# Splitting the operands of the block products on VectorE alone, the weights in whole raw tiles of 1024 columns

## The chip, the cores and the metric

The kernel runs on one core of a Trainium2 chip. Its engines work side by side, each on its own list of instructions in order: TensorE (PE in the profile, its weight loads PEld), VectorE (DVE), ScalarE (ACT), GpSimd (POOL) and SyncE (SP), whose queue here issues nearly all DMA transfers. The metric is the device time of one execution in microseconds (us); the time of a kernel is the median of its runs.

## The reference

Two layers over 1024 latent tokens of width 1024, with 256 context tokens that only the first layer needs. All is float32.

```python
# layer 0: z = h @ w_in, five parts of 1024 columns
y_a = conformer_conv(va, vg, p) * silu(ga)        # depthwise conv of 31 taps, LayerNorm, SiLU
y_b = rglru(xb, h_ctx) * silu(gb)                 # two recurrences, gates from 128x128 heads
x = x + gate * (concat([y_a, y_b]) @ w_out)
# layer 1: u, g = split(h @ w_in), 2048 columns each
d = multiscale_pool(u)                            # windows 2, 4, 8, 16 in rows of 64 tokens, minus u
y = einsum(d, w_grp) * scale                      # per group of 512 columns
x = x + gate * ((y * silu(g)) @ w_out)
return rmsnorm(x, final_g)
```

Before each layer stand an RMSNorm and a modulation by a shift and a scale. The kernel folds `w_grp` into the first half of layer 1's `w_in` (it calls the product `wfold`), and it keeps everything transposed: channels on the 128 partitions, tokens along the free axis in two halves of 512.

## The kernel before

**Three products for one.** Every float32 product is made of three TensorE products. A float32 operand is split into a high part, cast to the `float32r` type that TensorE multiplies, and a low part, the remainder. `split` (L94) does that with one ScalarE cast (L95) and one subtraction on a given engine (L96). Then hi*hi, hi*lo and lo*hi are summed in PSUM (L607, L609, L610). So each operand, weight or activation, costs one cast and one subtraction before TensorE can use it; the operands' engine is what this case is about.

**Block products.** From about the middle on the kernel multiplies by a 2x2 block scheme with seven products in place of eight. `wquad` (L569) prepares the weights of two output tiles of 128 columns at once. It loads two raw tiles of 128x1024 (tag `wr`, two buffers in all), sees them as four blocks a11, a12 and a21, a22 of 512 columns, forms sums of blocks on VectorE (L587, L588, L589, L595), partly in place, and splits seven operands p1 to p7, each from 512 columns. In the order of the code p1 and p6 are split on VectorE, and p5, p2, p7, p3, p4 on GpSimd. An operand's hi and lo parts share one tile of 128x1024. `quad` (L620) runs the products in the order p1, p5, p6, p2, p7, p3, p4 into three PSUM tiles a, c and b. `prod` (L603) makes 12 matmuls of 128x512 for each, so a quad has 84. Between the products `put` evacuates a PSUM tile, or a copy of it is kept, on ScalarE or VectorE, and the next product that adds into that tile waits for it. The factors on the token side (names b11, t1, t2, b21, t3, b22, t4) are sums of blocks too, split once and kept.

**Four uses, in the order of time.**

1. `woa` (names ending in `woa`): the half of layer 0's output projection that takes y_a, 4 quads. Its token operands are `ya_...`, split by `split_op` (L553), which takes VectorE for even i and GpSimd for odd i.
2. `v` and `g`, layer 1's input projection, for m = 0, 2, ..., 14: a quad of `wfold` weights (tiles `wq_v`) and one of `wg` weights (`wq_g`), 16 quads. Token operands `x_...` by `split_x` (L871); t1 and t4 on GpSimd, the others in a VectorE form of their own. Between them VectorE makes the pooling (`pool`, L928 to L946) of four half tiles, with 2, 4, 3 and 1 doubling steps for m = 0 and 2, 4 and 6, 8 and 10, 12 and 14. Then come the gating (L1062) and sums for the next operand (`block_sums`, L559 to L562), which are stored to memory.
3. `wo0`: the first part of layer 1's output projection, 4 quads (`wq_wo`). Its token operands `y_...` are read back from memory and split by `y_operand` (L971), each from 128x1024 columns: of a name's two tiles the first on GpSimd and the second on VectorE, except b22, both on VectorE.
4. `wo1`: the second part, 4 quads, the last two (names ending in `_l`, `late=True` in `wquad`) with the final RMSNorm worked in between.

**Buffers.** The weight operands of `v` and `g` live in the pool `xpool` (8 tiles of 128x1024), those of the other uses in a ring over the tags `wh`, `wl` (2 buffers each) and `d`. A tile is given out again when every reader of its last content is done. PSUM has 4 tiles for a, c and b.

**What sets the order.** The program is written as dataflow. A scheduler gives each engine's list its order by priorities and its own estimate of times, hands out the buffers as they come free and adds the waits. `tc.high_priority` moves evacuations ahead, and `tc.issue_after` holds some work back. A change of an operand's engine or size thus changes the order around it too.

Of the kernel before, what the change touches and what calls it, by code (L numbers as in the profile page):

```python
# [10 lines left out]
F32R = mybir.dt.float32r  # L11
# [4 lines left out]
P = 128  # L16
# [3 lines left out]
D = 1024  # L20
KT = D // P
H = 512
HALF = (slice(0, H), slice(H, S))
# [32 lines left out]
def body(ctx, tc, xT, ctxT, cc, ccol, modT, modW, win, gw, wout, wu, grp, wg, wo1, small, edge, ident, outT):  # L56
    nc = tc.nc
    mult, add, sub = ALU.mult, ALU.add, ALU.subtract
# [4 lines left out]
    wpool = ctx.enter_context(tc.tile_pool(name="wpool", bufs=2))  # L63
# [11 lines left out]
    def dtile(name, dt=F32):  # L75
        return dpool.tile([P, S], dt, tag="d", name=name)
# [4 lines left out]
    def ttile(name):  # L81
        return tpool.tile([P, H], F32, tag="t", name=name)
# [11 lines left out]
    def split(src, hi, lo, eng):  # L94
        return (nc.scalar.copy(hi, src),  # L95
                eng.tensor_tensor(out=lo, in0=src, in1=hi.bitcast(F32), op=sub))  # L96
# [161 lines left out]
    hh, hl, ch, cl = [], [], [], []  # L258
# [162 lines left out]
    with ExitStack() as actx:  # L421
# [6 lines left out]
        def ltile(name, dt=F32):  # L428
            return lpool.tile([P, E], dt, tag="l", name=name)
# [49 lines left out]
        for j in range(KT):  # L479
# [13 lines left out]
            w = wload(win[KT + j], f"vg{j}", nc.gpsimd)  # L493
            sg = []
            for h in range(2):
                ps = psum(f"vg{j}_{h}")
                mm3(ps, w, (hh, hl), HALF[h])
                t = ttile(f"sg{j}_{h}")
                nc.scalar.activation(t, ps, AF.Sigmoid)
                sg.append(t)  # L500
            w = wload(win[j], f"va{j}", nc.gpsimd)
# [13 lines left out]
            for d in range(2):  # L515
                for gi, ob in ((0, O_BR), (1, O_BI)):
                    kc = slice((2 * gi + d) * P, (2 * gi + d + 1) * P)
                    t = ltile(f"g{j}_{d}_{gi}")
# [21 lines left out]
    def vtile(name):  # L540
        return vpool.tile([P, H], F32, tag="v", name=name)
# [10 lines left out]

    def split_op(ops, name, i, src):  # L553
        hi, lo = ops[name]
        return split(src, hi[i], lo[i], nc.gpsimd if i % 2 else nc.vector)


    def block_sums(b11, b12, b21, b22, t3, eng):
# [10 lines left out]
    def wquad(src, name, ring, late=False):  # L569
        raw = []  # L570
        for i in range(2):
            r = wpool.tile([P, D], F32, tag="wr", name=f"wr_{name}_{i}")
            loaded[0] = nc.sync.dma_start(r, src[i])
            raw.append(r)
        a11, a12 = [raw[0][:, h] for h in HALF]
        a21, a22 = [raw[1][:, h] for h in HALF]

        def op(v, i, eng):
            t = ring(f"wq_{name}_{i}")
            split(v, t[:, HALF[0]], t[:, HALF[1]], eng)  # L580
            return t

        p1 = op(a11, 1, nc.vector)
        if late:
            p4 = op(a22, 4, nc.gpsimd)
        s3 = ttile(f"ws_{name}")
        nc.vector.tensor_tensor(out=s3, in0=a11, in1=a21, op=sub)  # L587
        nc.vector.tensor_tensor(out=a21, in0=a21, in1=a22, op=add)  # L588
        nc.vector.tensor_tensor(out=a11, in0=a21, in1=a11, op=sub)  # L589
        if not late:  # L590
            p5 = op(a21, 5, nc.gpsimd)
        p6 = op(a11, 6, nc.vector)
        p2 = op(a12, 2, nc.gpsimd)
        p7 = op(s3, 7, nc.gpsimd)
        nc.vector.tensor_tensor(out=a12, in0=a12, in1=a11, op=sub)  # L595
        if late:
            p5 = op(a21, 5, nc.gpsimd)
        p3 = op(a12, 3, nc.gpsimd)
        if not late:
            p4 = op(a22, 4, nc.gpsimd)  # L600
        return p1, p2, p3, p4, p5, p6, p7

    def prod(ps, w, op, first, last):  # L603
        xh, xl = op
        for k in range(KH):
            hi, lo = w[:, k * P : (k + 1) * P], w[:, H + k * P : H + (k + 1) * P]
            nc.tensor.matmul(ps, hi, xh[k], start=(first and k == 0), stop=False,  # L607
                             skip_group_check=not first)
            nc.tensor.matmul(ps, hi, xl[k], start=False, stop=False, skip_group_check=not first)  # L609
            mm = nc.tensor.matmul(ps, lo, xh[k], start=False, stop=(k == KH - 1),  # L610
                                  skip_group_check=not first)
        return mm
# [47 lines left out]
    for j in range(KT):  # L660
        w = wload(win[4 * KT + j], f"gb{j}", nc.gpsimd)
# [51 lines left out]
    for h in range(2):  # L713
        ps = wide(f"mu{h}", h)[:, :H]
        nc.tensor.matmul(ps, ones, lnacc[h][:, :H], start=True, stop=True)
        for j in range(KT):
            v = us[j][:, HALF[h]]
# [3 lines left out]
            else:  # L721
                q = ttile(f"lsq{j}_{h}")
                nc.scalar.activation(q, v, AF.Square)
                eng = nc.gpsimd if h else nc.vector
# [5 lines left out]
    for m in range(KT):  # L730
        w = wload(wout[m, 1], f"wob{m}", nc.gpsimd)
        for h in range(2):
            ps = psum(f"wob{m}_{h}")
            mm3(ps, w, (bh, bl), HALF[h])
            t = vtile(f"xp{m}_{h}")
            nc.sync.dma_start(t, xT[m][:, HALF[h]])
            with tc.high_priority(offset=EVAC):
                nc.vector.scalar_tensor_tensor(out=t, in0=ps, scalar=m0[:, 0, 2 * KT + m : 2 * KT + m + 1],
                                               in1=t, op0=mult, op1=add)
# [32 lines left out]
    for i in range(KH):  # L772
        for j in (i, KH + i):
            w = wload(win[2 * KT + j], f"ga{j}", nc.gpsimd)
            for h in range(2):
# [3 lines left out]
                v = us[j][:, HALF[h]]  # L779
                nc.vector.tensor_tensor(out=v, in0=v, in1=ps, op=mult)  # L780
        b11, b12 = [us[i][:, h] for h in HALF]
        b21, b22 = [us[KH + i][:, h] for h in HALF]
        split_op(ya, "b11", i, b11)
        split_op(ya, "b21", i, b21)
        t1, t2, t3, t4 = b11, ttile(f"yat2_{i}"), b12, b21
# [19 lines left out]
    def wo_weights(m):  # L805
        return wquad([wout[m + i, 0] for i in range(2)], f"woa{m}", ring_w)
# [49 lines left out]
    def ring_x(name):  # L856
        return xpool.tile([P, S], F32R, tag="x", name=name)

    first_ring = iter(["wh", "wl", "wh", "wl"])

    def ring_first(name):
        tag = next(first_ring, None)
        return dtile(name, F32R) if tag is None else wpool.tile([P, D], F32R, tag=tag, name=name)

    def v_weights(m, ring):
        return wquad([wfold[(m + i) // 4][(m + i) % 4].rearrange("p k c -> p (k c)") for i in range(2)], f"v{m}", ring)
# [4 lines left out]
    def split_x(name, i, src, shift, eng):  # L871
        hi, lo = bx[name]
        if shift is None:
            split(src, hi[i], lo[i], eng)
        else:
            nc.scalar.activation(hi[i], src, AF.Identity, bias=shift)
            nc.vector.scalar_tensor_tensor(out=lo[i], in0=src, scalar=shift, in1=hi[i].bitcast(F32), op0=add, op1=sub)
# [6 lines left out]
    def shift(k):  # L884
        return m1[:, 0, k : k + 1]
# [9 lines left out]
    for i in range(KH):  # L895
        b11, b21 = x1[i][:, HALF[0]], scaled(0, KH + i)
        split_x("b21", i, b21, shift(KH + i), None)
        b12, b22 = scaled(1, i), scaled(1, KH + i)
        t = block_sums(b11, b12, b21, b22, ttile(f"xt3_{i}"), nc.vector)
        split_x("t1", i, t["t1"], None, nc.gpsimd)  # L900
        split_x("t2", i, t["t2"], shift(KH + i), None)
        split_x("t3", i, t["t3"], dsh[:, i : i + 1], None)
        split_x("b22", i, b22, shift(KH + i), None)
        split_x("t4", i, t["t4"], None, nc.gpsimd)


    fin = [None, None]
# [63 lines left out]
    def y_operand(ops, part, name, raw_tile, alloc):  # L971
        hi, lo = [], []
        for q in range(2):
            r = raw_tile(f"yr_{part}_{name}_{q}")
            nc.sync.dma_start(r, y_raw[part][name][:, q * S : (q + 1) * S])
            hi.append(alloc(f"y{part}_{name}h{q}", F32R))
            lo.append(alloc(f"y{part}_{name}l{q}", F32R))
            split(r, hi[q], lo[q], nc.vector if q or name == "b22" else nc.gpsimd)
        halves = lambda ts: [t[:, h] for t in ts for h in HALF]
        ops[name] = halves(hi), halves(lo)  # L980

# [23 lines left out]
    for m in range(0, NK, 2):  # L1005
# [38 lines left out]
        elif m <= KT:  # L1044
            n = 2 * KT + m - 2
            for q in range(2):
                raw = dtile(f"mod1_{n + q}")
# [7 lines left out]
        w = quad(wq, f"g{m}", bx, to_gate, (lambda: wo1_weights(0, 0)) if m == NK - 2 else None)  # L1055
# [24 lines left out]
    for m in range(0, KT, 2):  # L1080
# [28 lines left out]
        w = quad(w, f"wo0_{m}", yops[0], put, nxt)  # L1109
# [10 lines left out]
    for m in range(0, KT - 4, 2):  # L1120
# [10 lines left out]
        w = quad(w, f"wo1_{m}", yops[1], put, ahead)  # L1131
# [99 lines left out]
    wb, _, _ = last_half0(m, wa, ahead)  # L1231
# [140 lines left out]
```

## Time and profile before

| what | value |
|---|---|
| median of 3 runs | 1459.48 us (1458.37 to 1459.95) |
| the profiled execution | 1463.59 us, its span 1461.8 us |
| busy in the span: PE, PEld | 1320.6 us (90%), 1060.1 us (73%) |
| busy in the span: DVE, ACT, POOL | 1220.5 us (83%), 653.0 us (45%), 695.8 us (48%) |
| mean granted TensorE clock | 0.959 |
| DMA | 181.79 MB, 124 GB/s over the span |

The profiled execution is one of its own: it took 4.1 us more than the median, and its span, from the first to the last instruction, is 1.8 us short of its time. Sums below are made against it. Busy time is a union, so what overlaps on one engine counts once. A group's mean mixes instructions that ran alone with those that something held up; the minimum, median and maximum of a tile's instructions tell the two apart. A wait is put down to the last semaphore that arrived.

### The profile page before, as it was taken

How to read it: one execution, taken by the hardware profiler on the slowest of the kernel's cores; microseconds unless marked ns; L12 is line 12 of the kernel's file. 1: busy time of each engine (PE TensorE's matmuls, PEld its weight loads, DVE VectorE, ACT ScalarE, POOL GpSimd, SP SyncE). 2: the span in 40 equal slices, each digit the busy share in tenths (PEclk: the TensorE clock that was granted, in tenths of full speed). 3: DMA queues.
4: the chain of work that ended last, by engine and by line, in shares of the span. 5: the costliest groups of instructions: out<-in, count | busy, mean ns of one | idle time of the engine just before them, and what ended most of it. 6: DMA issues, size and time to landing. Idle time of an engine off the chain costs nothing. (4 is left out here: it accounts for less than half of the span.)

```text
span 1461.8 us, 15776 instructions
## 1 busy us (share of the span) xinstructions
PE 1320.6 (90%) x5664; PEld 1060.1 (73%) x5664; DVE 1220.5 (83%) x1389; ACT 653.0 (45%) x928; POOL 695.8 (48%) x372
## 2 busy tenths in 40 slices
PE   7889989998899899999998998899889998889796
PEld 4478767776777677788886776677767777668585
DVE  7985889799879899997778749999999887876765
ACT  6343674475467623225424345533333334534442
POOL 5183644663666556424427435543243344654522
PEclk9899999999999999999999999999999999999998
DMA  9731112111211133443545364233323235647623
GB/s 354 253 121 37 65 37 73 51 68 40 79 51 51 64 103 106 142 141 115 168 159 174 121 194 131 86 115 131 127 75 108 101 108 137 234 162 266 237 73 115
DMA packets 82866, 181.79 MB, mean 124 GB/s; under 512 B 7778, under 2 KB 27618, under 8 KB 82788
## 3 DMA queue, kind: packets, MB, share of 16 engines
q1 hardware_dynamic: 74340, 176.60, 35.6%
q10 hardware_dynamic: 8448, 4.20, 1.0%
q8 instruction: 44, 0.72, 0.2%
q14 instruction: 34, 0.28, 0.1%
HBM read 136.72 MB, written 44.04 MB: 124 GB/s over the span
## 5 line engine op out<-in xcount | busy, mean ns | idle before, releaser
L688 DVE SCALAR_TENSOR_TENSOR conv<-u,sm,conv 128x1009 f32<-128x1009 f32 (+14 forms) x240 | 301.0, 1273 | 21.7 <-ACT conv L681 18.5
L96 POOL TENSOR_TENSOR wq_v<-wr_v,wq_v 128x512 fp32r<-128x512 f32 x32 | 54.3, 1712 | 84.6 <-ACT wq_v L95 84.4
L96 POOL TENSOR_TENSOR wq_g<-wr_g,wq_g 128x512 fp32r<-128x512 f32 x32 | 49.8, 1567 | 91.8 <-ACT wq_g L95 91.5
L96 POOL TENSOR_TENSOR wq_wo<-wr_wo,wq_wo 128x512 fp32r<-128x512 f32 x32 | 49.1, 1542 | 58.4 <-ACT wq_wo L95 48.6
L96 POOL TENSOR_TENSOR wl_wu<-wr_wu,wh_wu 128x1024 fp32r<-128x1024 f32 x16 | 39.4, 2467 | 73.6 <-ACT wh_wu L95 73.6
L95 ACT CAST wq_g<-wr_g 128x512 fp32r<-128x512 f32 x48 | 28.2, 619 | 94.7 <-DVE wr_g L588 33.9
L95 ACT CAST wq_v<-wr_v 128x512 fp32r<-128x512 f32 x48 | 28.2, 619 | 81.0 <-DVE wr_v L595 29.3
L521 PE MATMUL g<-uh,wh_gw 128*128 128x512 f32 (+1 forms) x96 | 40.7, 425 | 25.8 <-ACT g L524 16.3
L524 ACT ACTIVATE g<-g,sm 128x512 f32<-128x512 f32 (+1 forms) x96 | 53.6, 624 | 18.0 <-PE g L523 10.0
L440 POOL TENSOR_TENSOR g<-g,uc 128x1280 f32<-128x1280 f32 x16 | 47.4, 2961 | 19.6 <-ACT g L524 19.6
L243 PE MATMUL fold<-gh,wh_wu 128*128 128x512 f32 x128 | 52.7, 413 | 4.3 <-ACT wh_wu L95 4.3
L125 PE MATMUL gb<-h0h,wh_gb 128*128 128x512 f32 x128 | 51.2, 400 | 5.7 <-ACT sb L669 5.7
L244 PE MATMUL fold<-gl,wh_wu 128*128 128x512 f32 x128 | 52.5, 410 | 3.2 <-DVE gl L96 3.2
L95 ACT CAST wq_wo<-wr_wo 128x512 fp32r<-128x512 f32 x48 | 28.8, 619 | 58.9 <-DVE wr_wo L588 15.0
L445 POOL TENSOR_TENSOR g<-g,g 128x1280 f32<-128x1280 f32 x16 | 50.6, 3182 | 9.1 <-ACT g L444 9.1
L446 DVE SCALAR_TENSOR_TENSOR g<-a,g 128x1280 f32<-128x1280 f32 x16 | 37.1, 2317 | 20.4 <-POOL g L445 20.4
L245 PE MATMUL fold<-gh,wl_wu 128*128 128x512 f32 x128 | 50.9, 407 | 2.7 <-POOL wl_wu L96 2.7
L928 DVE TENSOR_TENSOR ws<-ws 128x616 f32<-128x616 f32 (+2 forms) x48 | 52.3, 1091 | 0.9
L458 POOL TENSOR_TENSOR g<-g,g 128x1024 f32<-128x1024 f32 x8 | 19.2, 2394 | 70.6 <-DVE g L455 70.6
L127 PE MATMUL va<-h0h,wl_va 128*128 128x512 f32 x128 | 49.5, 391 | 2.1 <-POOL wl_va L96 2.1
L126 PE MATMUL gb<-h0l,wh_gb 128*128 128x512 f32 x128 | 51.0, 399 | 0.0
L127 PE MATMUL gb<-h0h,wl_gb 128*128 128x512 f32 x128 | 50.8, 398 | 0.0
(566 smaller groups left out, 4744.7 us busy)
## 6 DMA issues: line engine op xcount, KB each, us to landing
mod<-modT SPq DMA_DIRECT2D x28, 512.0 KB, 5.3
wr_wu<-wu SPq DMA_DIRECT2D x16, 512.0 KB, 4.1
x_part<-xp SPq DMA_DIRECT2D x32, 256.0 KB, 2.6
mod<-modT SPq DMA_DIRECT2D x32, 256.0 KB, 3.3
wr_v<-wfold SPq DMA_DIRECT2D x16, 512.0 KB, 3.3
wr_g<-wg SPq DMA_DIRECT2D x16, 512.0 KB, 4.3
yr_t<-y_t SPq DMA_DIRECT2D x16, 512.0 KB, 6.1
wr_wo<-wo SPq DMA_DIRECT2D x16, 512.0 KB, 4.2
```

The source lines that it names most:

```text
L95: return (nc.scalar.copy(hi, src), eng.tensor_tensor(out=lo, in0=src, in1=hi.bitcast(F32), op=sub))
L96: eng.tensor_tensor(out=lo, in0=src, in1=hi.bitcast(F32), op=sub))
L125: nc.tensor.matmul(ps, hi[:, kc], xh[k][:, cols], start=(k == 0), stop=False)
L126: nc.tensor.matmul(ps, hi[:, kc], xl[k][:, cols], start=False, stop=False)
L127: nc.tensor.matmul(ps, lo[:, kc], xh[k][:, cols], start=False, stop=(k == ks - 1))
L243: nc.tensor.matmul(ps, wh[:, kc], gh[i], start=(i == 0), stop=False)
L244: nc.tensor.matmul(ps, wh[:, kc], gl[i], start=False, stop=False)
L245: nc.tensor.matmul(ps, wl[:, kc], gh[i], start=False, stop=(i == 3))
L445: nc.gpsimd.tensor_tensor(out=iu, in0=iu, in1=r, op=mult)
L524: nc.scalar.activation(t[:, a : a + n], ps[:, :n], AF.Sigmoid, bias=col(ob + d * KT + j))
L688: nc.vector.scalar_tensor_tensor(out=acp[:, a:b], in0=us[j][:, a + o : b + o], scalar=col(O_CONVW + 31 * j + k), in1=acp[:, a:b], op0=mult ...
L928: nc.vector.tensor_tensor(out=nxt[:, :, a_:b_], in0=cur[:, :, a_ + o0 : b_ + o0], in1=cur[:, :, a_ + o1 : b_ + o1], op=add)
```

## The change

All splits of the block products go to VectorE: `split_op`, the `x_t1` and `x_t4` splits, `y_operand`, and the weights in `wquad`. In `wquad` two operands are now split at once where two stand side by side in a raw tile. `both(1, raw[0])` splits the whole first raw tile into p1 and p2, `both(5, raw[1])` the second one into p5 and p4 after a21 + a22 has been formed in its first half, `both(6, raw[0])` the first tile again into p6 and p3 after both of its halves have been rewritten. Only p7 remains a split of 512 columns. The hi parts of such a pair share one tile of 128x1024 and the lo parts another, so a quad still takes seven tiles; a pair's tiles come free when both of its products are done. The two late quads keep seven splits of 512, on VectorE. The list of tags for the first quad of `v` is adapted.

```diff
     def split_op(ops, name, i, src):
         hi, lo = ops[name]
-        return split(src, hi[i], lo[i], nc.gpsimd if i % 2 else nc.vector)
+        return split(src, hi[i], lo[i], nc.vector)
 ...
-        def op(v, i, eng):
+        def op(v, i):
             t = ring(f"wq_{name}_{i}")
-            split(v, t[:, HALF[0]], t[:, HALF[1]], eng)
-            return t
-
-        p1 = op(a11, 1, nc.vector)
+            p = t[:, HALF[0]], t[:, HALF[1]]
+            split(v, *p, nc.vector)
+            return p
+
         if late:
-            p4 = op(a22, 4, nc.gpsimd)
+            p1, p4 = op(a11, 1), op(a22, 4)
+            s3 = ttile(f"ws_{name}")
+            nc.vector.tensor_tensor(out=s3, in0=a11, in1=a21, op=sub)
+            nc.vector.tensor_tensor(out=a21, in0=a21, in1=a22, op=add)
+            nc.vector.tensor_tensor(out=a11, in0=a21, in1=a11, op=sub)
+            p6, p2, p7 = op(a11, 6), op(a12, 2), op(s3, 7)
+            nc.vector.tensor_tensor(out=a12, in0=a12, in1=a11, op=sub)
+            p5, p3 = op(a21, 5), op(a12, 3)
+            return p1, p2, p3, p4, p5, p6, p7
+
+        def both(i, r):
+            hi, lo = [ring(f"wq_{name}_{i}{c}") for c in "hl"]
+            split(r, hi, lo, nc.vector)
+            return [(hi[:, h], lo[:, h]) for h in HALF]
+
+        p1, p2 = both(1, raw[0])
         s3 = ttile(f"ws_{name}")
         nc.vector.tensor_tensor(out=s3, in0=a11, in1=a21, op=sub)
         nc.vector.tensor_tensor(out=a21, in0=a21, in1=a22, op=add)
+        p5, p4 = both(5, raw[1])
         nc.vector.tensor_tensor(out=a11, in0=a21, in1=a11, op=sub)
-        if not late:
-            p5 = op(a21, 5, nc.gpsimd)
-        p6 = op(a11, 6, nc.vector)
-        p2 = op(a12, 2, nc.gpsimd)
-        p7 = op(s3, 7, nc.gpsimd)
         nc.vector.tensor_tensor(out=a12, in0=a12, in1=a11, op=sub)
-        if late:
-            p5 = op(a21, 5, nc.gpsimd)
-        p3 = op(a12, 3, nc.gpsimd)
-        if not late:
-            p4 = op(a22, 4, nc.gpsimd)
+        p6, p3 = both(6, raw[0])
+        p7 = op(s3, 7)
         return p1, p2, p3, p4, p5, p6, p7
 ...
-            hi, lo = w[:, k * P : (k + 1) * P], w[:, H + k * P : H + (k + 1) * P]
+            hi, lo = [v[:, k * P : (k + 1) * P] for v in w]
 ...
-    first_ring = iter(["wh", "wl", "wh", "wl"])
+    first_ring = iter(["wh", "wl", "d", "d", "d", "d", "wh"])
 ...
-        split_x("t1", i, t["t1"], None, nc.gpsimd)
+        split_x("t1", i, t["t1"], None, nc.vector)
 ...
-        split_x("t4", i, t["t4"], None, nc.gpsimd)
+        split_x("t4", i, t["t4"], None, nc.vector)
 ...
-            split(r, hi[q], lo[q], nc.vector if q or name == "b22" else nc.gpsimd)
+            split(r, hi[q], lo[q], nc.vector)
```

**In the order: VectorE at the weights of the g quad of m = 6.** `wr_g` are its raw tiles, `ws` and `vp` belong to the pooling, and the two rows that read `qb_v` and `qc_v` evacuate PSUM tiles of the v quad that TensorE adds into again (L1022 before, L1031 in the changed file). Before:

```order
L589 TENSOR_TENSOR wr_g_0_7583<-wr_g_1_7585,wr_g_0_7583 128x512
L928 TENSOR_TENSOR ws_0_1_7623<-vp_6540 128x8x79
L96 TENSOR_TENSOR wq_g_6_7597<-wr_g_0_7583,wq_g_6_7597 128x512
L928 TENSOR_TENSOR ws_0_2_7625<-ws_0_1_7623 128x8x77
L928 TENSOR_TENSOR ws_0_4_7627<-ws_0_2_7625 128x8x73
L595 TENSOR_TENSOR wr_g_0_7583<-wr_g_0_7583 128x512
L928 TENSOR_TENSOR ws_0_8_7629<-ws_0_4_7627 128x8x65
L937 TENSOR_TENSOR ws_0_8_7629<-ws_0_8_7629,eg 128x8x8
L941 TENSOR_TENSOR ws_0_8_7629<-ws_0_8_7629,eg 128x8x7
L946 SCALAR_TENSOR_TENSOR vp_6540<-ws_0_8_7629,vp_6540 128x8x64
L1022 TENSOR_TENSOR vp_6549<-qb_v_7480,s_v_7506 128x8x64
L1022 TENSOR_TENSOR vp_6543<-qc_v_7479,s_v_7520 128x8x64
```

And now, with the splits of whole raw tiles (`wq_g_1l`, `wq_g_5l`, `wq_g_6l`):

```order
L96 TENSOR_TENSOR wq_g_1l<-wr_g_0_7517,wq_g_1h 128x1024
L561 TENSOR_TENSOR y_7229<-y_7230,y_7229 128x512
L937 TENSOR_TENSOR ws_0_1_7551<-vp_6510 128x8x79
L606 TENSOR_TENSOR wr_g_0_7517<-wr_g_1_7519,wr_g_0_7517 128x512
L562 TENSOR_TENSOR y_7230<-y_7230,y_7229 128x512
L96 TENSOR_TENSOR wq_g_5l<-wr_g_1_7519,wq_g_5h 128x1024
L1031 TENSOR_TENSOR vp_6513<-qc_v_7413,s_v_7454 128x8x64
L937 TENSOR_TENSOR ws_0_2_7553<-ws_0_1_7551 128x8x77
L607 TENSOR_TENSOR wr_g_0_7517<-wr_g_0_7517 128x512
L1031 TENSOR_TENSOR vp_6519<-qb_v_7414,s_v_7440 128x8x64
L937 TENSOR_TENSOR ws_0_4_7555<-ws_0_2_7553 128x8x73
L96 TENSOR_TENSOR wq_g_6l<-wr_g_0_7517,wq_g_6h 128x1024
```

The two evacuations stand ahead of most of the pooling's chain now, where a whole pass of it (four sums, two edges, L946) stood ahead of them; between them stand the splits.

**GpSimd at the same place.** Before, its list held five rows for that quad:

```order
L96 TENSOR_TENSOR wq_g_5_7594<-wr_g_1_7585,wq_g_5_7594 128x512
L96 TENSOR_TENSOR wq_g_2_7600<-wr_g_0_7583,wq_g_2_7600 128x512
L96 TENSOR_TENSOR wq_g_7_7603<-ws_g_7590,wq_g_7_7603 128x512
L96 TENSOR_TENSOR wq_g_3_7607<-wr_g_0_7583,wq_g_3_7607 128x512
L96 TENSOR_TENSOR wq_g_4_7610<-wr_g_1_7585,wq_g_4_7610 128x512
```

Now it holds none from the last fold weight (`wl_wu`) and eight memsets to the last multiplications of the final norm (L1201):

```order
L96 TENSOR_TENSOR wl_wu_3_6107<-wr_wu_3_6104,wh_wu_3_6106 128x1024
L1020 MEMSET vp_6513 128x8x8
L1021 MEMSET vp_6513 128x8x8
L1020 MEMSET vp_6516 128x8x8
L1201 TENSOR_TENSOR o_0_10158<-x_1_9591,rr_10123 128x512
```

All five splits of that quad, and those of every other, have left GpSimd.

**TensorE at the start of `woa`.** Before, after the last matmuls of p1 (`wq_woa_1`) came the first two of p5, then of p6, then of p2:

```order
L610 MATMUL qa_woa_5490<-ya_b11h_4748,wq_woa_1_5423 128x512
L607 MATMUL qc_woa_5491<-ya_t1h_4751,wq_woa_5_5430 128x512
L609 MATMUL qc_woa_5491<-ya_t1l_4753,wq_woa_5_5430 128x512
L607 MATMUL qb_woa_5492<-ya_t2h_4755,wq_woa_6_5433 128x512
L609 MATMUL qb_woa_5492<-ya_t2l_4757,wq_woa_6_5433 128x512
L607 MATMUL qa_woa_5490<-ya_b21h_4759,wq_woa_2_5436 128x512
```

Now p1 is followed by all twelve of p2, from the same two tiles, and then by p5:

```order
L619 MATMUL qa_woa_5484<-ya_b11h_4748,wq_woa_1l 128x512
L616 MATMUL qa_woa_5484<-ya_b21h_4759,wq_woa_1h 128x512
L618 MATMUL qa_woa_5484<-ya_b21l_4761,wq_woa_1h 128x512
...
L619 MATMUL qa_woa_5484<-ya_b21h_4760,wq_woa_1l 128x512
L616 MATMUL qc_woa_5485<-ya_t1h_4751,wq_woa_5h 128x512
L618 MATMUL qc_woa_5485<-ya_t1l_4753,wq_woa_5h 128x512
L619 MATMUL qc_woa_5485<-ya_t1h_4751,wq_woa_5l 128x512
```

So twelve matmuls that need no further operand stand between p1 and p5 there.

4 lines of the change are left out of this document (2 added, 2 removed).

## The prediction

> **What bounds the kernel now.** First the page's head, then the table of stretches, cut at the first product of woa, v, the second v quad pair, the last two pairs, wo0 and the late quads:
>
> ```profile
> span 1461.8 us, 15776 instructions
> 765.00:862.00 97.00, 87.31 (x362) 69.29 (x360) 71.39 (x73) 40.52 (x68) 53.08 (x32) 0.95 0.45 148
> 908.40:951.20 42.80, 34.67 (x134) 26.61 (x133) 40.39 (x46) 25.18 (x43) 23.53 (x21) 0.92 0.25 80
> 951.20:1165.40 214.20, 197.02 (x841) 158.93 (x840) 197.80 (x268) 72.40 (x131) 81.59 (x50) 0.98 0.33 112
> 1165.40:1262.30 96.90, 86.88 (x362) 70.09 (x361) 77.18 (x88) 37.57 (x63) 44.84 (x25) 0.95 0.45 138
> 1262.30:1396.30 134.00, 116.27 (x481) 93.46 (x480) 97.73 (x91) 57.36 (x86) 70.21 (x39) 0.95 0.63 216
> 1396.30:1461.00 64.70, 52.36 (x251) 43.11 (x249) 41.73 (x66) 22.88 (x42) 19.98 (x17) 0.89 0.28 98
> ```
>
> After the stretch's length come the busy times of PE, PEld, DVE, ACT and POOL. PE looks 90% busy, but a matmul's row overlaps the next, so I go by starts:
>
> ```profile
> 1040.03 0.39 PE L607 MATMUL qb_g<-x_t3h,wq_g 128*128 128x512 f32 x1
> 1040.25 0.39 PE L609 MATMUL qb_g<-x_t3l,wq_g 128*128 128x512 f32 x1
> 1040.48 0.39 PE L610 MATMUL qb_g<-x_t3h,wq_g 128*128 128x512 f32 x1
> ```
>
> One matmul per 0.2265 us is PE's pace, so a quad of 84 (the code's count; records can be missing) needs 19.0 us and a v, g pair 38.05. Above that floor: woa, 4 quads, 97.0 - 76.1 = 20.9; the first pair 42.8 - 38.05 = 4.7; the next five pairs 214.2 - 190.3 = 23.9; the last two 96.9 - 76.1 = 20.8; six wo quads 134.0 - 114.2 = 19.8. Together 90 us in which PE, the bound of this half, stood still or ran slow. The waits of PE from 765 us on name whom it waited for:
>
> ```profile
> PE qb_wo L607 <- DVE s_wo L1092: 11.3, 3, 6.2
> PE qb_g L607 <- ACT qb_g L625: 9.6, 3, 4.2
> PE qb_v L607 <- DVE vp L1022: 7.0, 2, 3.9
> PE qb_g L610 <- DVE wq_g L96: 4.7, 2, 3.0
> PE qc_woa L607 <- ACT wq_woa L95: 4.6, 1, 4.6
> PE qb_wo L607 <- DVE x L1077: 4.5, 1, 4.5
> PE qb_g L607 <- ACT wq_g L95: 4.2, 2, 3.6
> ```
>
> Mostly VectorE is late with an evacuation or an operand, or ScalarE, which itself waits for VectorE's sums. One such wait, on both lists, and the clock behind it:
>
> ```profile
> 1023.69 0.23 DVE L937 TENSOR_TENSOR ws<-ws,eg 128x64 f32<-128x64 f32 x1
> 1023.83 1.28 DVE L941 TENSOR_TENSOR ws<-ws,eg 128x56 f32<-128x56 f32 x1
> 1025.15 1.66 DVE L946 SCALAR_TENSOR_TENSOR vp<-ws,vp 128x512 f32<-128x512 f32 x1
> 1026.73 0.68 DVE L1022 TENSOR_TENSOR vp<-qb_v,s_v 128x512 f32<-128x512 f32 x1
> ```
> ```profile
> 1027.47 0.79 PE L607 MATMUL qb_v<-x_t4h,wq_v 128*128 128x512 f32 x1 [3.88 <-DVE vp L1022]
> ```
> ```profile
> 1027.40:1030.80 3.40, 3.33 (x8) 0.50 0.53 172
> 1030.81:1034.20 3.39, 3.39 (x17) 1.00 0.00 0
> ```
>
> An edge product of 56 columns takes 1.28 us, where one of 64 took 0.23, L946 takes 1.66, and PE stands for 3.88 us. Then the granted clock is 0.50 for 3.4 us and 8 matmuls pass instead of 15 to 17, another 1.7 us. What is late in those rows is a collision with GpSimd:
>
> ```profile
> L96 POOL TENSOR_TENSOR wq_g<-wr_g,wq_g x32: 1262/1630/1933, 935.2 to 1242.3; 128x512 fp32r<-128x512 f32 x32
> L96 DVE TENSOR_TENSOR wq_g<-wr_g,wq_g x16: 679/693/1777, 924.3 to 1236.4; 128x512 fp32r<-128x512 f32 x16
> L595 DVE TENSOR_TENSOR wr_g<-wr_g x8: 683/1756/1778, 940.6 to 1238.3; 128x512 f32<-128x512 f32 x8
> ```
> ```profile
> 1040.93 0.80 DVE L928 TENSOR_TENSOR ws<-ws 128x616 f32<-128x616 f32 x1
> 1041.60 1.29 POOL L96 TENSOR_TENSOR wq_v<-wr_v,wq_v 128x512 fp32r<-128x512 f32 x1 [2.46 <-ACT wq_v L95]
> 1041.65 1.78 DVE L96 TENSOR_TENSOR wq_v<-wr_v,wq_v 128x512 fp32r<-128x512 f32 x1
> 1053.47 0.69 DVE L96 TENSOR_TENSOR wq_g<-wr_g,wq_g 128x512 fp32r<-128x512 f32 x1
> ```
>
> Minimum, median and maximum: the same 512-column instruction takes VectorE 0.69 us or about 1.77, little between; the long form stands beside a running GpSimd split.
>
> **The change part by part.** *Collisions removed.* A GpSimd split costs VectorE up to 1.77 - 0.69 = 1.08 us. In the five middle pairs 50 of them ran, up to 54 us of VectorE's 197.8 busy; I take that whole price, since a GpSimd row lasts longer than VectorE's and nearly always meets one. Its bounds are 0 and 1.29 each, the unhindered GpSimd row.
>
> *Splits added.* For 1024 columns both engines have a row:
>
> ```profile
> L96 POOL TENSOR_TENSOR y_b11l<-yr_b,y_b11h x2: 2722/2756/2789, 1230.7 to 1307.1; 128x1024 fp32r<-128x1024 f32 x2
> L96 DVE TENSOR_TENSOR y_b11l<-yr_b,y_b11h x2: 1207/1208/1209, 1240.0 to 1315.6; 128x1024 fp32r<-128x1024 f32 x2
> ```
>
> A quad's VectorE splits go from 2 x 0.69 = 1.38 to 3 x 1.21 + 0.69 = 4.32, so +2.94; 26 quads, 76 us. The two late quads get five of 0.69 more, 3.5 each. Added operand splits: 14 of `ya` and 8 of `x` at 0.69, 12 of `y` at 1.21: 30 us. That is 113 us of work, against 174 GpSimd splits gone. In the middle pairs VectorE's list becomes 197.8 - 54 + 10 x 2.94 = 173 us, 34.6 a pair under PE's 38.05. The five average 3.2 doubling steps on four half tiles; with four steps (m = 4, 6) it is 3.2 sums more, of 0.80 (row at 1040.93), 37.2: level with PE there, and below it elsewhere.
>
> *Casts.* Seven of 0.62 become three of 1.05 and one of 0.62 (rows below), 0.57 us less per quad on an engine busy for a third of the stretch: nothing.
>
> ```profile
> L95 ACT CAST wq_g<-wr_g x48: 602/620/627, 922.0 to 1240.6; 128x512 fp32r<-128x512 f32 x48
> L95 ACT CAST wh_wu<-wr_wu x16: 1038/1049/1058, 12.4 to 884.9; 128x1024 fp32r<-128x1024 f32 x16
> ```
>
> *Raw tiles come free earlier.* No load is moved or added, but SP's weight loads wait for the raw tiles, and the chain of waits runs through that:
>
> ```profile
> 1177.63 1.30 POOL wq_v L96
> 1178.95 4.14 DMA wr_g<-wg
> 1183.85 0.69 DVE wq_g L96
> ```
>
> GpSimd's last split freed the raw tile, and 4.14 us of load followed. Now VectorE's third whole split frees it, after 1.21 us and not after five splits of 1.3 to 1.9. I price it inside the stages' terms.
>
> *Operand tiles come free later.* With pairs, p5's tiles are held until p4, the quad's last product. The next quad gets its tiles from p1/p2, p3/p6 and the spare one, and between the first product after p3 and the next p5 stand about 24 matmuls, 5.4 us. A split takes 1.21 of it, so VectorE may be some 4 us late before this costs anything.
>
> *Longer instructions.* The first operand is ready after 1.05 + 1.21 = 2.26 us instead of 0.62 + 0.69 = 1.31. Nothing among the waits quoted is for a quad's first product; in woa p2 now follows p1 for 12 x 0.2265 = 2.7 us, more than the 0.95 lost. I take zero.
>
> The Trainium skill (Perfetto Trace Analysis, Optimizing Scalar/DVE Operations) says the opposite of this edit: where VectorE is not saturated but causes bubbles, breaking instructions up may let work finish sooner. By it each of 26 quads would lose 0.95 us, 25 in all, and the time would be 1447. No run here shows which holds; the waits quoted speak for zero.
>
> **The sum, by stage.** woa: the 4.6 us at the start and the slow clock behind it, for which p2 now gives cover: -8 (bounds 0 to -17). First pair: `x` operands and fold still crowd VectorE: -1 (+4 to -5). Five pairs: of 23.9 above the floor, 13 go; the two pairs where VectorE is level with PE keep most of theirs (-4 to -24). Last two pairs, with the read-back of `y` and its splits in series: -7 (0 to -15). wo: waits of 11.3 and 4.5 behind a hindered VectorE list, but 14.5 us of `y` splits come in: -8 (+2 to -15). Before 765 us and after 1396 us nothing. Together -37, so 1463.6 - 37 = 1426.6 for the profiled execution. That one was 4.1 above the median of 1459.5, which puts the forecast at 1422 us, with bounds +2 to -76: 1461 to 1384.
>
> **Rivals.**
> *VectorE remains the bound.* It is busy for 92% of the middle stretch and takes over another engine's work; its list has less in it but also serves evacuations behind 1.21 us splits. For it: the level pairs. Against it: 34.6 against 38.05 on the average. Then only a third of the 37 is won: 1447. The skill's section named above warns that VectorE and GpSimd share a read port, so moving work between the two might not help; that too would end here.
> *Slower: the tile pairs starve TensorE.* If VectorE is more than 4 us late at a quad's end, p5 finds no tile. A stall like the one at 1027 us, here of 3 us with 1.5 of slow clock, in half of the 26 paired quads is 13 x 4.5 = 58 against the 37 won: 1459.5 + 21 = 1480. It decides from the ninth such stall on. Against it: the 4 us of slack, and VectorE rows without long forms.
> *TensorE's floor.* If all stalls at VectorE go: about 1388. Against it: first weights, read-back and norm have chains of their own.
> *It does nothing.* Were the long rows due to something else than GpSimd, 113 us of new work would fill what the move leaves: 1459. Against it: the rows at 1041 us.
>
> **How the numbers follow.** Forecast 0.55 (its own range 1400 to 1442), VectorE the bound 0.16, slower 0.13, floor 0.08, nothing 0.08. About 0.2%, 2.9 us, is what a measurement can tell from no change. Faster by more: 0.55 + 0.16 + 0.08 = 0.79; slower: 0.13 and a share of the last, 0.14; the rest 0.07. The range from 1390 to 1460 leaves out most of the slower case and half of the floor, some 0.17.
>
> **What would show it.** No VectorE row of 512 columns near 1.77 us after the fold; its whole splits at 1.21; PE's waits on `vp`, `s_wo` and `wq_woa` gone or short; fewer stretches at clock 0.50; the five pairs near 201 us. Wrong: new waits of p5 or p6 on `wq` operands with VectorE busy ahead of them, or a VectorE list over 190 us in the middle stretch.

## The result, and the profile after

The changed kernel takes 1404.45 us, the median of 4 runs (1404.10 to 1405.26); the kernel before, beside it on the same chip, 1459.72 us (1458.37 to 1461.64). The ratio is 0.9621, with a 95% interval of 0.9605 to 0.9638: 55 us or 3.8% faster. The forecast was 1422, its range 1390 to 1460. The profiled execution took 1404.68 us, its span is 1402.9, so the sums below (58.9 us between two spans) are 3.6 us larger than the difference of the medians.

The head of the page of the changed kernel, its busy times and the row of GpSimd in 40 slices of 35 us:

```profile
span 1402.9 us, 15463 instructions
PE 1298.8 (93%) x5664; PEld 1050.4 (75%) x5664; DVE 1169.2 (83%) x1485; ACT 644.2 (46%) x850; POOL 398.7 (28%) x198
POOL 5173726754564655633320004000000000000002
```

VectorE took over 174 splits and is busy for 1169.2 us, 51 us less than before. GpSimd has next to nothing to do between the fold and the end (0.7 us of memsets). The stretches answer to those in the prediction, cut at the same products (woa, norm and fold, first pair, five pairs, last two pairs, wo, late quads); after the length stand PE, PEld, DVE, ACT and POOL, then the granted clock:

```profile
762.40:850.80 88.40, 83.05 (x362) 67.04 (x360) 65.03 (x88) 37.57 (x55) 5.51 (x3) 1.00 0.48 161
850.80:892.60 41.80, 41.80 (x188) 34.06 (x189) 31.22 (x43) 23.56 (x36) 14.29 (x8) 1.00 0.69 201
892.60:930.90 38.30, 33.60 (x146) 26.73 (x146) 37.64 (x60) 25.26 (x40) 0.70 (x6) 1.00 0.28 90
930.90:1124.00 193.10, 193.10 (x853) 159.91 (x852) 180.72 (x299) 70.67 (x101) 0.00 (x0) 1.00 0.37 124
1124.00:1203.80 79.80, 76.36 (x338) 62.91 (x336) 58.29 (x83) 32.24 (x44) 0.00 (x0) 0.99 0.48 149
1203.80:1342.60 138.80, 125.57 (x504) 99.08 (x505) 99.22 (x123) 60.46 (x77) 0.00 (x0) 0.93 0.65 218
1342.60:1402.00 59.40, 46.84 (x227) 38.52 (x225) 39.25 (x68) 19.24 (x37) 8.04 (x9) 0.90 0.32 106
```

The middle stretch has 853 matmuls in 193.10 us, 0.2264 us each: TensorE doesn't stand still there any more, and its clock is 1.00. A cut of this kind has a trap, though. The list order changed, so 12 or 24 matmuls of a neighbouring stage (2.7 or 5.4 us) now stand on the other side of a cut: wo has 504 of them where it had 481, and its 138.8 us against 134.0 aren't a loss. The fair measure is a stage's length less its matmuls (by their starts in the trace) times 0.2265. In us:

| stage | above its matmuls, before | after | gain | forecast |
|---|---|---|---|---|
| up to woa (its length) | 765.1 | 762.4 | 2.7 | 0 |
| woa | 15.6 | 6.8 | 8.8 | 8 |
| norm and fold (some narrower matmuls) | 3.6 | -0.7 | 4.3 | 0 |
| first pair | 12.8 | 5.6 | 7.2 | 1 |
| five pairs | 24.0 | 0.1 | 23.9 | 13 |
| last two pairs | 15.3 | 3.7 | 11.6 | 7 |
| six wo quads | 25.3 | 24.7 | 0.6 | 8 |
| late quads and end | 8.8 | 9.1 | -0.3 | 0 |

The gains add up to 58.8 us, the difference of the spans but for rounding. The 2.7 us up to woa aren't explained: there the kernels of the experiments lie between 761.1 and 764.9 us. The groups of VectorE's splits and sums in the five pairs (minimum, median and maximum in ns):

```profile
L96 DVE TENSOR_TENSOR wq_g_1l<-wr_g,wq_g_1h x5: 1214/1218/1220, 949.4 to 1099.9; 128x1024 fp32r<-128x1024 f32 x5
L607 DVE TENSOR_TENSOR wr_g<-wr_g x5: 677/681/684, 955.5 to 1104.8; 128x512 f32<-128x512 f32 x5
```

L607 is the sum that was L595 before; its median there was 1756 ns, here 681, and no long form is left in the five pairs. What TensorE still waits for from 765 us on:

```profile
PE qa_wo L616 <- DVE xp L1086: 4.1, 2, 3.1
PE fin_ms L1174 <- DVE fin L1166: 3.7, 2, 2.0
PE qa_wo L616 <- ACT wq_wo_1h L95: 3.4, 1, 3.4
PE qb_v L616 <- ACT qb_v L634: 3.1, 1, 3.1
PE qc_wo L616 <- ACT s_wo L662: 2.9, 2, 2.5
PE qa_wo L619 <- DVE wq_wo_1l L96: 1.8, 2, 1.2
```

The waits that the prediction quotes are gone or short (`s_wo` on VectorE 0.9 us where it was 11.3). The largest row is a new one, for `xp`. What is left lies mostly in wo, and two rows of it name the operand of a pair, `wq_wo_1h` and `wq_wo_1l`.

### The profile page after: what moved, and what is told of

It reads as the page before. It is cut to its first block, busy times and chain, and to the rows that moved or that the text cites. A ratio compares the mean times of both kernels' runs of the same rounds, so it can differ in the third digit from the quotient of the medians.

```text
span 1402.9 us, 15463 instructions
## 1 busy us (share of the span) xinstructions
PE 1298.8 (93%) x5664; PEld 1050.4 (75%) x5664; DVE 1169.2 (83%) x1485; ACT 644.2 (46%) x850; POOL 398.7 (28%) x198
## 4 chain that ended last, share of the span: by engine, by line
PE 44%; DVE 28%; DMA 10%; ACT 8%; issue 6%; POOL 3%; SPq 0%; POOLq 0%; DVEq 0%; ACTq 0%
DVE conv L697 9%; DMA x_part<-xp 3%; DVE g L455 2%; PE wob L125 2%; PE wob L126 2%; PE wob L127 2%; PE qb_v L618 1%; PE qb_v L619 1%; PE qb_v L616 1%; DVE junk L206 1%; PE qb_g L618 1%; PE qb_g L619 1%; PE qb_g L616 1%; DMA xp<-x_part 1%; DMA wr_wu<-wu 1%
## 5 line engine op out<-in xcount | busy, mean ns | idle before, releaser
L1201 POOL TENSOR_TENSOR o<-x,rr 128x256 f32<-128x256 f32 (+1 forms) x9 | 8.0, 928 | 470.9 <-ACT fq L1160 468.0
L524 ACT ACTIVATE g<-g,sm 128x512 f32<-128x512 f32 (+1 forms) x96 | 53.8, 621 | 17.7 <-PE g L523 9.8
L126 PE MATMUL wob<-ybl,wh_wob 128*128 128x512 f32 x128 | 50.3, 394 | 0.0
L127 PE MATMUL ga<-h0h,wl_ga 128*128 128x512 f32 x128 | 50.2, 392 | 0.0
L125 PE MATMUL wob<-ybh,wh_wob 128*128 128x512 f32 x128 | 50.0, 394 | 0.1
L127 PE MATMUL xb<-h0h,wl_xb 128*128 128x512 f32 x128 | 50.0, 391 | 0.0
L127 PE MATMUL wob<-ybh,wl_wob 128*128 128x512 f32 x128 | 49.9, 393 | 0.0
L125 PE MATMUL xb<-h0h,wh_xb 128*128 128x512 f32 x128 | 49.9, 390 | 0.0
L126 PE MATMUL xb<-h0l,wh_xb 128*128 128x512 f32 x128 | 49.9, 390 | 0.0
```

The source lines that it names most:

```text
L125: nc.tensor.matmul(ps, hi[:, kc], xh[k][:, cols], start=(k == 0), stop=False)
L126: nc.tensor.matmul(ps, hi[:, kc], xl[k][:, cols], start=False, stop=False)
L127: nc.tensor.matmul(ps, lo[:, kc], xh[k][:, cols], start=False, stop=(k == ks - 1))
L524: nc.scalar.activation(t[:, a : a + n], ps[:, :n], AF.Sigmoid, bias=col(ob + d * KT + j))
```

## The experiments

The theory on record: GpSimd's splits held VectorE up (collisions), and the change takes that away. The rivals: the pairs are the gain; or GpSimd was merely slow in handing over its operands. Then come the questions that the profile after raised: why wo won nothing, and what the pairs are worth. The kernel before ran beside each group of experiments, with medians of 1459.8 to 1461.9 us. Where a few us decide, the differences of the medians and those of the ratios (times 1460 us) are both given, since they come out up to 3 us apart.

**Separate splits, no pairs.** The kernel before with every splitting engine replaced:

```diff
-            p5 = op(a21, 5, nc.gpsimd)
+            p5 = op(a21, 5, nc.vector)
 ...
-        p2 = op(a12, 2, nc.gpsimd)
-        p7 = op(s3, 7, nc.gpsimd)
+        p2 = op(a12, 2, nc.vector)
+        p7 = op(s3, 7, nc.vector)
```

> The kernel before with every split of the block products' operands on VectorE, but seven separate ones of 512 columns per quad, as it had them: no pairs. Collision theory (the long VectorE rows beside GpSimd's splits were the loss): nearly the whole gain of the change comes, about 1404 to 1415 us; VectorE's list is longer than the changed kernel's by 7 x 0.69 - 4.32 = 0.5 us per quad, and the raw tiles come free a little later. Pairing theory (whole splits, fewer casts and earlier free raw tiles are the gain): most of the gain is missing, 1430 to 1450 us. VectorE's 512-column rows at 0.69 us after the fold in both cases.

Measured: 1390.06 us (1389.02 to 1394.77), ratio 0.952 (0.9504 to 0.9536). The collision theory's direction, and below its range: this is faster than the changed kernel, whose interval lies wholly above. So the whole gain and 14 us beyond it come from the engine alone, and the pairs cost these 14 us (15 by the ratios). They were forecast at zero or a small gain. By stages (us above the matmuls, in a profiled execution 4.7 us above the median): first pair 2.3 against 5.6 with pairs, five pairs 1.8 against 0.1, last two 0.5 against 3.7, wo 16.9 against 24.7. The difference lies in wo and in the first and the last pairs, not in the middle stretch.

**Extra reads by GpSimd, and extra writes as a control.** Both add work to the changed kernel whose result nobody reads:

```diff
+    def extra(hi, lo):
+        nc.gpsimd.tensor_tensor(out=cX, in0=hi.bitcast(F32), in1=lo.bitcast(F32), op=sub)
 ...
             split(r, hi, lo, nc.vector)
+            for h in HALF:
+                extra(hi[:, h], lo[:, h])
```

and for the control, in place of the subtraction:

```diff
+        nc.gpsimd.tensor_copy(out=cX[:, :8], in_=lo[:, :8].bitcast(F32))
+        for _ in range(2):
+            nc.gpsimd.memset(cX, 0.0)
```

> The changed kernel with work added: after each whole split GpSimd subtracts two 512-column halves into a tile that nobody reads, six such instructions per paired quad in all, where the kernel before had five GpSimd splits. They read the operand tiles from SBUF and nothing waits for them. Collision theory: VectorE's rows with two SBUF inputs grow from 0.69 to up to 1.77 again; in the five middle pairs VectorE's list goes from 181 us to 225 to 245 and becomes the bound, that stretch grows by 30 to 50 us, and the whole comes out at 1445 to 1490 us. Theory that GpSimd was only slow in handing over operands: nothing waits for these instructions, so 1404 us within 4.

> The control to the kernel with extra reads: at the same places GpSimd copies 8 columns and then fills 512 columns twice, so it writes SBUF and reads next to nothing. If reading SBUF is what holds VectorE up: 1404 us within 4, VectorE's 512-column rows at 0.69. If any work of GpSimd does it: slower in proportion to GpSimd's busy time, as the kernel with extra reads.

Measured: with reads 1484.88 us, ratio 1.0168 (1.0153 to 1.0183), 1.7% slower than the kernel before; with writes 1402.53 us, ratio 0.9611 (0.9593 to 0.9629), as without. The five pairs of the two traces, reads first, in the columns of the stretches above:

```profile
940.20:1184.40 244.20, 210.94 (x853) 168.04 (x852) 240.99 (x305) 70.82 (x101) 117.16 (x62) 0.94 0.29 99
```
```profile
929.70:1122.80 193.10, 193.10 (x853) 159.96 (x852) 180.86 (x299) 70.75 (x101) 117.89 (x182) 1.00 0.37 124
```

GpSimd is busy for the same time in both, 117 and 118 us. In the control 64 us of that are 122 fills, which only write; 54 us are 60 copies of 8 columns, whose rows last 0.19 to 4 us. The instructions that read two operands of 512 columns lengthen VectorE's list from 180.9 to 241.0 us, about 1.0 us for each of the 62 in the stretch; the fills and the small copies lengthen it by nothing. With 241 us in 244 VectorE is the bound. VectorE's groups with reads, then the same form with writes (busy us, mean ns):

```profile
L1077 DVE SCALAR_TENSOR_TENSOR y<-vp,sm,y 128x512 f32<-128x512 f32 x21 | 25.2, 1198 | 0.2
```
```profile
L1079 DVE SCALAR_TENSOR_TENSOR y<-vp,sm,y 128x512 f32<-128x512 f32 x20 | 14.9, 745 | 0.2
```

And one meeting in the list of the kernel with reads:

```profile
1037.61 3.69 POOL L571 TENSOR_TENSOR cH<-wq_v_1h,wq_v_1l 128x512 f32<-128x512 f32 x2 [9.00 <-DVE wq_v_1l L96]
1037.65 0.81 DVE L943 TENSOR_TENSOR ws<-vp 128x632 f32<-128x632 f32 x1
1038.38 1.78 DVE L1077 SCALAR_TENSOR_TENSOR y<-vp,sm,y 128x512 f32<-128x512 f32 x1
```

The gating instruction of 0.745 us takes 1.78 beside two GpSimd reads that take 1.85 each, where the GpSimd split alone took 1.29 in the kernel before. So both sides pay. GpSimd's share can be large: single rows of this read last from 1.26 to 5.06 us. No engine waits for these reads in the trace (in the control ScalarE waits 17 us for tiles that the copies still hold, and the stretch is no longer for it), so collisions cost time by themselves, without any slow operand. Slow operands in the kernel before aren't excluded by that, but its trace leaves them little room: none of TensorE's waits from 765 us on names an operand from GpSimd. What stays open is the release of the raw tiles. In the five pairs SyncE waited 94.5 us for GpSimd's splits (`wq_g` and `wq_v`) before it could load the next weights; in the waits of TensorE there, evacuations (`vp` and `qb_g`) have 12.4 us and split weights 4.5. No run moved the release alone, so its share of the gain isn't known. The Trainium skill (SBUF — State Buffer, Who interferes with whom) states that a VectorE instruction with two SBUF inputs contends with a GpSimd instruction that reads SBUF and not with one that only writes it. These two runs agree; the price, about 1.0 us of VectorE per 512-column read, is from the trace.

**One extra read per quad.** The same edit, behind the first whole split only and for one half:

> The changed kernel with one extra GpSimd read per paired quad instead of six (512 columns, after the first whole split; nobody waits for it). With six, VectorE's list in the five middle pairs grew by 60 us in 244. If each read costs VectorE about 1.0 us and only the sum of the list counts: 181 + 10 = 191 us in the middle stretch, still under TensorE's 193, so that stretch stays within 2 us and the whole comes out at 1404 to 1409 us. If single collisions already hit evacuations that TensorE waits for: the middle stretch grows by 5 to 10 us and the whole by 12 to 26, 1416 to 1430.

Measured: 1410.5 us, ratio 0.9654 (0.9634 to 0.9673). The middle stretch:

```profile
932.10:1130.80 198.70, 195.82 (x854) 159.16 (x854) 188.70 (x298) 71.13 (x101) 29.69 (x10) 1.00 0.36 121
```

VectorE's list grew by 8.0 us for ten reads, to 188.7, still less than TensorE's 193, and yet the stretch grew by 5.6. The whole is just above the range of the theory that only the sum of the list counts (4.8 us by the ratios, 6.0 by the medians), and well below the other one's; the stretch alone is as that other theory has it, 5 to 10 us. So a sum below the bound doesn't hide every collision. TensorE's waits in the stretch, 2.9 us, name `wq_g_5l`, `wq_v_5l` and `vp`; the other 2.7 us have no row, and which of the ten reads cost something wasn't followed.

**Token operands back on GpSimd.** The changed kernel with `split_op`, the `x_t1` and `x_t4` splits and `y_operand` as they were before.

> The changed kernel, but the splits of the token operands (14 of ya, 8 of x, 12 of y) go back to GpSimd, as in the kernel before; the weights keep their pairs on VectorE. Collision theory: these 34 GpSimd splits hold VectorE up only around 765 us, around 900 us and in wo, so a few us are lost: 1406 to 1414 us. Theory that the added operand splits on VectorE are what kept wo from gaining: wo falls from 138.9 to about 131, 1396 us.

Measured: 1416.52 us, ratio 0.9687 (0.9666 to 0.9707), 12 us slower than the change (10 by the ratios) and a little above the collision theory's range. So these 34 splits on GpSimd cost about 0.3 us each, and the weights alone bring 43 to 46 of the 55 us. The theory that the y splits on VectorE kept wo from gaining fails: with them on GpSimd wo is at 27.8 us above its matmuls, not lower. The run brings the collisions of these splits back too, so it doesn't give the weight of the y splits by themselves. Norm and fold stay at -0.7, so what that stage won is from the weights.

**Four xp tiles in flight.** In the wo0 quads `put` loads a tile `xp` of x1_part, adds the product and stores it again, through a pool of two buffers. The waits of SyncE's queue in the wo stretch, in the changed kernel and then in the kernel before:

```profile
SPq L1097 <- DMA x_part<-xp: 38.1, 10, 8.7
SPq L1104 <- DVE xp L1086: 13.2, 9, 4.7
```
```profile
SPq L1095 <- DVE xp L1077: 39.0, 16, 8.1
SPq L1088 <- DMA x_part<-xp: 11.4, 9, 2.8
```

Before, the queue waited for VectorE (the store for the sum). After, it waits for the store itself, before the next load into that tile can go: 38.1 us against 11.4. The chain of waits of the changed kernel runs through it (start, duration):

```profile
1302.28 4.81 DMA x_part<-xp
1307.11 4.50 DMA xp<-x_part
1311.69 0.76 DVE xp L1086
1312.59 0.77 PE qa_wo L616
```

A store of 4.81 us, a load of 4.50, then VectorE's addition, and behind it in VectorE's list the next quad's first split; TensorE stands for 3.1 us there. VectorE's additions (L1086) stood idle for such loads, in the changed kernel and then in the one with separate splits (us, times):

```profile
  DMA xp<-x_part: 12.4, 5
```
```profile
  DMA xp<-x_part: 6.3, 4
```

The edit takes every other tile from the pool of the pooling's sums:

```diff
+    xp_n = [0]
+
+    def xp_tile(name):
+        xp_n[0] += 1
+        return vtile(name) if xp_n[0] % 2 else atile(name)[:, :H]
 ...
-            t = vtile(f"xp{m}_{i}_{h}")
+            t = xp_tile(f"xp{m}_{i}_{h}")
```

> The changed kernel, but the tiles xp of the wo quads of the first half of y come from two pools in turn, so four of them are in flight instead of two. The changed kernel's wo stretch takes 138.8 us against a floor of 114 and won nothing; its SyncE queue waits 38.1 us there for stores of x_part before it may load the next xp. Theory that this round trip through memory bounds wo now: the stretch falls by 8 to 18 us, 1386 to 1396 us. Rival, that VectorE's added y splits (14.5 us) eat the gain in wo: no change, 1404 us within 3.

Measured: 1396.9 us, ratio 0.9565 (0.955 to 0.9579), 7.5 us faster (8 by the ratios); wo at 17.6 us above its matmuls instead of 24.7. VectorE's additions wait for no load any more (12.4 us before), TensorE's waits for `xp` (4.1 and 1.7 us) are gone, and SyncE's wait for `x_part` falls from 38.1 to 17.7 us. So the round trip held wo up by some 7 us, and the time stayed just above the range that I gave. The other 17.6 us have other causes.

**Both together.** Separate splits and four xp tiles.

> Both edits that were faster than the changed kernel: seven separate splits per quad on VectorE (1390.1 us alone) and four xp tiles in flight (7.6 us off the changed kernel). If they act on different waits: 1380 to 1385 us. If separate splits had already taken the wait for x_part (SyncE's waits for it are 21.6 us with them, 38.1 in the changed kernel): no more than 2 us, 1388 to 1391.

Measured: 1391.03 us, ratio 0.9515 (0.9491 to 0.9538), which can't be told from separate splits alone. It fits that the two act on one wait: with separate splits SyncE's wait for `x_part` is shorter without any new tile (the wo stretch of that kernel), and the new tiles take it only to 19.3 us:

```profile
SPq L1095 <- DVE xp L1077: 24.5, 16, 4.8
SPq L1088 <- DMA x_part<-xp: 21.6, 13, 3.9
```

**Pairs, with the instructions halved.** What of the 14 us is the length of instructions, and what the pairs' tiles and order?

```diff
-            split(r, hi, lo, nc.vector)
+            for h in HALF:
+                split(r[:, h], hi[:, h], lo[:, h], nc.vector)
```

> The changed kernel with its pairs of tiles, its order and its lifetimes, but each whole split is given as two of 512 columns, first operand first. If the length of the instructions (2.26 us until the first operand, 1.21 us that an evacuation waits behind) is what pairing costs: close to the kernel with separate splits, 1388 to 1394 us. If it is the pairs' tiles and the order of the splits: 1403 to 1408 us, with 0.5 us per quad more on VectorE.

Measured: 1398.16 us, ratio 0.956 (0.9541 to 0.9579), between the two ranges. Halving takes 6 us off (9 by the ratios), although VectorE has more to do, and wo falls to 16.9 us above its matmuls, the value of separate splits; VectorE's additions wait 7.0 us for loads of `xp` there, close to the 6.3 of separate splits. So shorter instructions shorten the round trip's wait without a new tile. The first pair is at 7.0 and the last two at 5.1, no lower than with whole splits, where separate splits have 2.3 and 0.5. So length is about half of the pairs' cost (6 of 14 us, or 9 of 15 by the ratios); the rest goes with their tiles and order, and which of these two wasn't tried.

**Only the first pair halved.**

```diff
-            split(r, hi, lo, nc.vector)
+            if i == 1:
+                for h in HALF:
+                    split(r[:, h], hi[:, h], lo[:, h], nc.vector)
+            else:
+                split(r, hi, lo, nc.vector)
```

> The changed kernel with only the first pair of each quad (p1 and p2) split in two instructions of 512 columns, p1 first; the other two pairs whole. Halving all three pairs took 6.3 us off the changed kernel, with wo at 16.9 us above its matmuls instead of 24.7. If the wait for a quad's first operand (2.26 us of cast and split, 1.31 in halves) is the cost of whole instructions: nearly all of the 6 us, 1397 to 1400. If it is what queues behind the 1.21 us splits and 1.05 us casts at any place: about a third, 1401 to 1403.

Measured: 1400.36 us, ratio 0.9573 (0.9544 to 0.9602), between the ranges, and its interval (1395 to 1404 us) holds both in full. By the medians the first operand has 4 of the 6 us, by the ratios 7 of the 9; that leans to it but doesn't settle it.

**y in halves.** The trace of the kernel with both edits still has a wait of 3.1 us for a copy on ScalarE in wo, with y casts of 1.05 us ahead of it. Here that kernel's y splits are halved.

```diff
-            split(r, hi[q], lo[q], nc.vector)
+            for h in HALF:
+                split(r[:, h], hi[q][:, h], lo[q][:, h], nc.vector)
```

> The kernel with seven separate splits per quad and four xp tiles (1391.0 us), and the read-back y split as two instructions of 512 columns each instead of one of 1024, on ScalarE and VectorE. In its trace TensorE still stands 3.2 us in wo for a copy on ScalarE that is queued behind y casts of 1.05 us, and the wo quads are 14.7 us above their matmuls. Theory that long instructions in front of evacuations are what wo loses: 2 to 5 us less, 1386 to 1389 us. If it is the loads of y that are late: 1391 within 2.

Measured: 1392.03 us, ratio 0.9538 (0.9515 to 0.9562), no gain; the wait is 3.2 us. The edit halved the length of a cast but not the work ahead of the copy: in the new trace y casts of 512 columns still fill most of ScalarE's list from 1288.8 to 1293.1 us, and the copy starts at 1294.1. So the length of one cast isn't the cause; whether the copy's place in the list is wasn't tried.

**Halved pairs in woa only, separate splits elsewhere.**

> Seven separate splits per quad on VectorE everywhere (1390.1 us) except in woa, where the pairs in halves were better (3.5 us above the matmuls against 7.3). If stages add up: 1386 to 1388 us. If what woa gains is given back by the fold's first weights, which wait for loads: 1390 within 1.5.

Measured: 1394.65 us, ratio 0.9536 (0.9511 to 0.9562): no gain over separate splits. woa did come to 3.9 us above its matmuls instead of 7.3, but the first pair went from 2.3 to 6.7. Stages don't add up here: what an early one won, the next lost. Where it lost it wasn't followed.

## Why the prediction was right, and where it wasn't

**The cause: right.** Collisions were named as what is late in the waits, at a price of up to 1.08 us. The extra reads show 1.0 us each, the fills nothing, and the long rows are gone. In the trace of the kernel before, every VectorE `TENSOR_TENSOR` of 512 columns that took over 0.75 us between 765 and 1396 us (70 of 273) overlaps a GpSimd row, and none of the 141 that overlap no such row took that long. Against the medians of the same forms in the changed kernel and with separate splits, VectorE's rows of the five pairs are 47 us longer, nearly all of it in 46 rows, for 50 GpSimd splits; I had taken 54. "It does nothing" and "a transfer of work to a busy VectorE can't help" fall with that: splits that I put at 113 us came in, and VectorE's busy time is still 51 us shorter, so what it lost in collisions was the larger part. The Trainium skill's caution (Perfetto Trace Analysis, Optimizing Scalar/DVE Operations), that the two engines share a read port and moving work between them might not help, didn't hold for this move.

**The five pairs: right in kind, too small.** I let 13 of 24 us go, because two pairs where VectorE is level with TensorE would keep their stalls. None did: 0.1 us is left. VectorE's list came to 180.7 us, not 173. The collisions gave back 47 us and not 54, and the list has 11 instructions (6 us) more than the 268 + 20 that I counted, work of neighbouring stages that now falls between the cuts. A list of 94% of the stretch was no hindrance with nothing late in it; the term should have stood at its bound of 24.

**Norm, first pair, last two pairs: too small** (0, 1 and 7 forecast, 4.3, 7.2 and 11.6 measured). I kept these stalls for loads, read-back and fold. The collisions there had the same long forms, which I didn't count: VectorE's rows were longer than without GpSimd by 6 us in norm and fold, 12 in the first pair and 24 in the last two. With the token operands back on GpSimd, the first pair loses 3.3 us of its gain and the last two 2.0, and norm and fold lose none; the rest is the weights'.

**wo: wrong.** Forecast -8, measured -0.6. The step that failed is "the waits of 11.3 and 4.5 behind a hindered VectorE list" as the limit of that stage. They went, and the round trip of `xp` through two buffers came in their place: VectorE's additions waited 5.1 us for its loads before and 12.4 after. It was in the trace before, as 11.4 us of SyncE's waits behind the 39.0 for VectorE, and I didn't follow the queue that far. Separate splits get just these 8 us (25.3 to 16.9), halved pairs too, four xp tiles 7.7. So the wait needs both, two buffers and the long splits. What makes up the 15 to 18 us that are left in each of these kernels stays open.

**Longer instructions: wrong.** "I take zero" was the term, on the ground that none of the quoted waits was for a quad's first product. Those were the waits of the kernel before; after the change two of the six rows are for exactly that operand. Halving the instructions wins 6 to 9 us, and the pairs as a whole cost 14. The Trainium skill's rule (Perfetto Trace Analysis, Optimizing Scalar/DVE Operations), that breaking instructions up may let work finish sooner where an engine isn't saturated but causes bubbles, has the sign that the trace shows. The 25 us that I worked out beside it was three to four times too large, as if most quads hid the 0.95 us; which ones do wasn't measured.

**Operand tiles that come free later.** I gave them 4 us of slack and zero. No stall of the size named in the slower rival appeared in the trace after, but 6 to 8 us of the pairs' cost aren't length; the tiles' lifetimes may be in it. That isn't shown.

So the total came out 18 us better than forecast, 22 between the two profiled spans: the terms up to the last two pairs were too small by 29, and wo was too hopeful by 7. The time lies within the range with errors of both signs in the sum: the direction and the mechanism were foreseen, but that the 7 us missing in wo were more than covered elsewhere was luck.

## What to carry to other kernels

Before a split or sum goes to GpSimd "because it is idle", look for two lengths of the same VectorE instruction: if the long one stands beside GpSimd instructions that read SBUF, the busy engine pays for the idle one's work, and the work may cost less on the busy engine itself. Change the engine and the grouping in separate runs: here the first won 70 us and the second lost 14, and only their sum was to be seen. When the wait ahead of a stage goes, read the DMA queue's own waits for the next one in line.

## What the runs showed of the hardware that I had not expected

GpSimd's fills cost VectorE nothing: 122 of them, 64 us in a stretch of 193, with 54 us of copies of 8 columns, left VectorE's list at 180.9 us. The collision also reaches VectorE's three-operand form when two of its inputs are tensors in SBUF (0.745 to 1.198 us in the mean). GpSimd pays too: its read of 512 columns, 1.26 us at the shortest, takes up to 5.06 us in the kernel with six reads per quad and 1.7 to 5.2 in the one with a single read. And a VectorE list with 4.4 us in 193 to spare can already delay TensorE: ten reads, which lengthened it by 0.8 us each, cost the stretch 5.6.
